# A warm-up of zeros, an attention's parts in another order, softmax steps in pairs and unpadded diagonal blocks

## The chip, the cores and the metric

The kernel runs on one core of a Trainium2 chip. The metric is the device time of one execution in microseconds (us); smaller is better. The engines are TensorE (PE, its weight loads PEld), VectorE (DVE), ScalarE (ACT), GpSimd (POOL) and SyncE (SP, which only starts DMAs). They run side by side and wait for each other through semaphores.

## The reference

512 tokens of width 1024 go through three stages in float32. A first block with attention and a wide FFN, a gated linear attention (GLA) and a sparse attention with selected keys (DSA). What the change touches:

```
# first block
u = rmsnorm(h, g_mix_pre); z = u @ w_in        # w_in also holds the latents q_lat, kv_lat and k_rope
q = rmsnorm(q_lat) @ w_q_up; kv = rmsnorm(kv_lat) @ w_kv_up      # 8 heads of 64 + 32 (rope), v of 64
q_pe, k_pe = rope(q_pe), rope(k_rope)
ob = softmax(mask(q_full k_full^T * scale)) v                    # mask by chunks of 64
ya = (a_b * conv3(a_c * a_x)) @ w_a_out                          # the branch called conv_a
...
# second block, layer 0: GLA, 4 heads, q, k of 256, v of 512
S = S * decay + k^T v; o = q S + (lower triangle of q k^T) v
# second block, layer 1: DSA, 16 heads of 128, one key and one value for all
logits = (q k^T) * ATTN_SCALE on the 128 selected keys of each query
o = softmax(logits) v
# behind each layer
x = layer_norm(ALPHA * x + y); x = x + (p @ ple_w) * sigmoid(x @ ple_gate_w)
```

## The kernel before

All activations lie transposed, features on partitions and 512 tokens in the free dimension, in eight tiles X[:, c, :]. A product in float32 is made of three matmuls in fp32r: each operand is split into a high part (a rounded copy, made by ACT) and a low part (the rest, made by DVE), and PE adds hi x hi, hi x lo and lo x hi (`part`, `mm3`, the L245 and L264 to L266 rows). Weights come as slabs of 128 x 1024 floats through four buffers called raw, and are split into whi and wlo in the same way. PSUM has banks for four uses: mm (3), s (2), t (2) and o (1).

PE's instructions stand in the order in which the code writes them. The other engines' instructions are put in order by a scheduler, so an edit of PE's order moves rows on DVE, ACT and POOL too. SP, ACT and POOL each issue DMAs in their own order.

**The start.** Five loads of X and of w_lat alternate on SP's queue; vec (all small vectors, 128 x 281) goes through ACT's. ACT makes XH as X times the gain column of vec, DVE makes XL. The latents need 72 matmuls, nine for each of the eight chunks.

**The first attention.** `Stream` holds the 24 half-steps of conv_a, 12 matmuls of 512 columns each, and `fill.run(n)` puts n of them between the attention's parts. kr is the key's rope part, r_u, rq and rk are reciprocal roots for 512 tokens, computed in [128, 4] tiles by chains of small DVE steps, and spread() brings such a tile into rows with transposes on PE. `mla_k` and `mla_q` make keys and queries of two heads, `mla_r` the rotated part of four heads' queries, which goes through DRAM (qrh, qrl) back into the tiles Qh and Ql by POOL's DMAs. `mla_s(h, t)` makes the scores of a query block t of 128, its maximum mx, the bias nb, the exponential p with its sum sm (ACT), the reciprocal and, on POOL, p times it. `soft_t` transposes p into bank t and splits it into pthi and ptlo, `mla_av` multiplies with V. The loop over eight heads does the transposes of head h, the scores of head h+1 and fill in turn.

**The padded blocks.** The last query block needs 128 columns. `weighted()` gives it 256 (three matmuls), with zeros ahead of it, and so do the scores of the first block in DSA:

```
c0 = min(j, 2) * 128
n = max(256, (t + 1) * 128)
```

**The tail.** The last tile of the last gate is computed at full width and then treated in two halves.

Of the kernel before, what the change touches and what calls it, by code (L numbers as in the profile page):

```python
# [96 lines left out]
def program(tc, a, out, upto=99):  # L97
# [72 lines left out]
    class Slab:  # L170


        def __init__(self, ap, cols):
            self.cols, self.parts = cols, []
            self.step = 512 if cols % 384 else 384
            self.raw = wp.tile([128, 1024], F32, name="raw", tag="raw", bufs=4)
            with tc.high_priority(offset=AHEAD):
                nc.sync.dma_start(self.raw[:, :cols], ap)

        def split(self, n=2):  # L180

# [100 lines left out]
    drp = top.enter_context(tc.tile_pool(name="drp", bufs=1, space=bass.MemoryType.DRAM))  # L282
    vec = cp.tile([128, NVEC], F32, name="vec")
# [8 lines left out]

    copy(cp.tile([128, 1], F32, name="warm"), ones)
# [8 lines left out]
    X = cp.tile([128, DC, S], F32, name="X")  # L302
# [159 lines left out]
    def weighted(ps, m, vs, pt):  # L462
# [6 lines left out]
    def soft_exp(p_, src, scale, nb, sm, eng=dve):  # L469

        act.activation(p_, src, AF.Exp, bias=nb, scale=scale, accum_out=sm)
        dve.reciprocal(sm, sm)
        eng.tensor_scalar(p_, p_, sm, None, op0=OP.mult)

    def soft_t(p_, t, pt):

        n = (t + 1) * 128
        ps = bank("t")
        for j in range(t + 1):
            pe.transpose(ps[:, j * 128:(j + 1) * 128], p_[:, j * 128:(j + 1) * 128], ident)  # L480
        pv = ps[:, :n].rearrange("p (j c) -> p j c", c=128)
        hi, lo = pt_view(pt[0], t), pt_view(pt[1], t)
# [75 lines left out]
    xin, w_in = a["xT"], a["w_in"]  # L558

    w_first = []  # L560
    for c0, c1 in ((0, 1), (1, 2), (2, 4), (4, 6), (6, 8)):
        with tc.high_priority(offset=AHEAD):
            nc.sync.dma_start(X[:, c0:c1, :], xin[:, c0 * S:c1 * S].rearrange("p (a b) -> p a b", b=S))
        w = slab(a["w_lat"][:, c0 * 384:c1 * 384], (c1 - c0) * 384)
        for i in range(c0, c1):
            split(XH[:, i, :], XL[:, i, :], X[:, i, :], vcol("g_mix_pre", i))
# [138 lines left out]
    fill.run(4)  # L705


# [3 lines left out]

    V = ap_.tile([128, NB, 8, 128], F32R, name="V")
    wv = slab(a["w_kv_v"], 1024)
    for b in range(NB):
        ps = bank("s" if b % 2 else "mm")
        bl = slice(b * 128, (b + 1) * 128)
        mm3(ps, [((kvn[k][0][:, bl], kvn[k][1][:, bl]),
                  wv(k * 512, 512)) for k in range(2)])
        split(V[:, b, :, 0:64], V[:, b, :, 64:128], ps[:, :].rearrange("p (h c) -> p h c", c=64), rk[:, b:b + 1])

# [32 lines left out]
    def mla_s(h, t):  # L753
        (qh, ql), (kh, kl) = QT[h % 2], KT[h % 2]
        if t == 0:
            MX[h] = [small(n_ + str(h % 2)) for n_ in ("mx", "nb", "sm")]
        mx, nb, sm = (x[:, t:t + 1] for x in MX[h])
        bl = slice(t * 128, (t + 1) * 128)
        n = max(256, (t + 1) * 128)
        ps_ = bank("s")  # L760
        pe.matmul(ps_[:, :n], qh[:, bl], kh[:, :n], start=True, stop=False)
        pe.matmul(ps_[:, :n], qh[:, bl], kl[:, :n], start=False, stop=False)
        pe.matmul(ps_[:, :n], ql[:, bl], kh[:, :n], start=False, stop=True)
        n = (t + 1) * 128
        dve.tensor_reduce(mx, ps_[:, :n], AX.X, OP.max)
        mul(nb, mx, nsrq[:, t:t + 1])
        p_ = PR[h, t] = ap_.tile([128, n], F32, name=f"p{t}", tag=f"p{t}")
        soft_exp(p_, ps_[:, :n], srq[:, t:t + 1], nb, sm, gps)
# [16 lines left out]
    mla_k(0)  # L785
    mla_q(0)
    fill.run(1)
    for t in range(NB):
        mla_s(0, t)
        if t == 1:  # L790
            mla_r(1)
# [911 lines left out]
```

## Time and profile before

| what | value |
|---|---|
| median of the runs | 1760.61 us (1759.82 to 1761.05, 3 runs) |
| the profiled execution | 1759.98 us |
| its span | 1758.2 us |
| PE busy | 1738.3 us, 8845 matmuls |
| DVE, ACT, POOL busy | 1207.0, 900.9, 86.6 us |
| first matmul | 5.96 us |
| PE's waits from 37 to 175 us | 7.6 us |

The span is what the profiler saw from the first to the last instruction; the time of the execution is 1.8 us longer. Ends of matmuls are modelled, since they are pipelined: how fast PE goes is read from the distance of the starts.

### The profile page before, as it was taken

The page shows a single profiled execution, that of the slowest core. Times are in us where ns is not written, and L with a number is a line of the kernel's source. Part 1 is how long each engine was busy: PE and PEld are TensorE (multiplying, and loading weights), DVE is VectorE, ACT ScalarE, POOL GpSimd, SP SyncE. Part 2 cuts the span into 40 slices and gives each one's busy share as a digit, 9 for nine tenths or more (in the row PEclk, how much of TensorE's full clock was granted, in tenths as well). Part 3 has the DMA queues.
Part 4 walks back from the last instruction along what each step waited for, and adds up shares of the span by engine and source line. Part 5 has one row for each costly group of instructions (what it writes and reads, how often), then busy time and mean ns, then how long its engine had stood idle before and what let it go on. Part 6 is the DMA issues. An engine that isn't in the chain of part 4 may idle for free.

```text
span 1758.2 us, 24149 instructions
## 1 busy us (share of the span) xinstructions
PE 1738.3 (99%) x8845; PEld 1464.7 (83%) x8845; DVE 1207.0 (69%) x2710; ACT 900.9 (51%) x1708; POOL 86.6 (5%) x147
## 2 busy tenths in 40 slices
PE   8899999999999999999999999999999999999998
PEld 6688888898888888899888888888988888888897
DVE  6987545488727657688554464556979988888885
ACT  6466433356434434455773744733765356444454
POOL 0455000000000000000000000000000000000000
PEclk9999999999999999999999999999999999999999
DMA  5322322213323232333312322232232321221231
GB/s 200 95 85 73 120 96 96 96 61 120 96 96 93 75 108 87 99 118 123 103 59 67 96 84 84 73 126 91 80 126 72 97 84 61 61 73 61 66 103 60
DMA packets 50758, 160.99 MB, mean 92 GB/s; under 512 B 5888, under 2 KB 7168, under 8 KB 50640
## 3 DMA queue, kind: packets, MB, share of 16 engines
q1 hardware_dynamic: 49328, 157.41, 27.5%
q0 software_dynamic: 1024, 1.64, 0.4%
q8 instruction: 69, 1.13, 0.3%
q14 instruction: 49, 0.40, 0.1%
q10 hardware_dynamic: 288, 0.41, 0.1%
HBM read 153.14 MB, written 4.72 MB: 90 GB/s over the span
## 4 chain that ended last, share of the span: by engine, by line
PE 96%; DVE 2%; ACT 1%; DMA 1%; issue 0%; SPq 0%; DVEq 0%; ACTq 0%
PE ps_mm L245 72%; PE ps_s L245 7%; PE ps_o L467 2%; PE ps_mm L264 2%; PE ps_mm L266 2%; PE ps_mm L265 2%; PE ps_t L480 1%; PE ps_s L467 1%; PE ps_t L1215 1%; PE ps_t L378 1%; PE ps_s L1161 1%; PE ps_o L777 1%; PE ps_s L264 1%; PE ps_s L265 1%; PE ps_s L266 1%; PE ps_t L340 0%
## 5 line engine op out<-in xcount | busy, mean ns | idle before, releaser
L116 ACT ACTIVATE whi<-raw 128x512 fp32r<-128x512 f32 (+1 forms) x551 | 337.4, 621 | 444.9 <-PE ps_mm L245 371.0
L245 PE MATMUL ps_mm<-XH,whi 128*128 128x512 f32 (+1 forms) x1376 | 522.9, 380 | 6.7 <-ACT whi L116 6.0
L245 PE MATMUL ps_mm<-XH,wlo 128*128 128x512 f32 (+1 forms) x1376 | 523.4, 380 | 0.2 <-DVE up L116 0.2
L245 PE MATMUL ps_mm<-XL,whi 128*128 128x512 f32 (+1 forms) x1376 | 522.0, 379 | 0.0
L116 DVE TENSOR_TENSOR wlo<-raw,whi 128x512 fp32r<-128x512 f32 (+2 forms) x549 | 368.7, 680 | 169.9 <-ACT whi L116 165.9
L245 PEld LDWEIGHTS ps_mm<-XH,whi 128*128 128x128 f32 x1376 | 259.9, 189 | 57.3 <-ACT whi L116 6.0
L245 PEld LDWEIGHTS ps_mm<-XL,whi 128*128 128x128 f32 x1376 | 260.0, 189 | 52.6
L245 PEld LDWEIGHTS ps_mm<-XH,wlo 128*128 128x128 f32 x1376 | 260.0, 189 | 51.7 <-PE ps_o L245 0.6
L116 ACT ACT_TABLE_LOAD x62 | 79.5, 1283 | 10.5 <-DVE nb L116 3.7
L116 DVE SCALAR_TENSOR_TENSOR upt<-up,vec,upt 128x511 f32<-128x511 f32 (+1 forms) x88 | 65.4, 749 | 10.9 <-ACT upt L116 9.7
L245 PE MATMUL ps_mm<-fh,wlo 128*128 128x512 f32 (+1 forms) x153 | 55.9, 365 | 0.0
L245 PE MATMUL ps_mm<-fh,whi 128*128 128x512 f32 (+1 forms) x153 | 55.8, 365 | 0.0
L245 PE MATMUL ps_mm<-fl,whi 128*128 128x512 f32 (+1 forms) x153 | 55.8, 365 | 0.0
L245 PE MATMUL ps_s<-XL,whi 128*128 128x256 f32 (+2 forms) x176 | 51.9, 295 | 0.7 <-DVE XL L116 0.7
L245 PE MATMUL ps_s<-XH,wlo 128*128 128x256 f32 (+2 forms) x176 | 51.8, 294 | 0.0
L245 PE MATMUL ps_s<-XH,whi 128*128 128x256 f32 (+2 forms) x176 | 51.4, 292 | 0.0
L116 DVE TENSOR_TENSOR up<-ps_mm,RU 128x512 f32<-128x512 f32 x41 | 28.2, 690 | 33.4 <-PE ps_mm L245 33.4
L266 PE MATMUL ps_mm<-whi,XL 128*128 128x512 f32 x128 | 50.6, 395 | 0.0
L264 PE MATMUL ps_mm<-whi,XH 128*128 128x512 f32 x128 | 50.6, 395 | 0.0
L265 PE MATMUL ps_mm<-wlo,XH 128*128 128x512 f32 x128 | 50.6, 395 | 0.0
L245 PE MATMUL ps_mm<-dth,wlo 128*128 128x512 f32 (+1 forms) x128 | 48.4, 378 | 0.0
L245 PE MATMUL ps_mm<-pthi,wlo 128*128 128x512 f32 (+1 forms) x128 | 48.2, 377 | 0.0
(506 smaller groups left out, 3217.2 us busy)
## 6 DMA issues: line engine op xcount, KB each, us to landing
raw<-in_w_ffn_up SPq DMA_DIRECT2D x44, 512.0 KB, 3.4
raw<-in_dsa_w SPq DMA_DIRECT2D x38, 512.0 KB, 3.5
raw<-in_w_in SPq DMA_DIRECT2D x31, 512.0 KB, 3.3
raw<-in_gla_qk SPq DMA_DIRECT2D x16, 512.0 KB, 4.3
raw<-in_gla_z SPq DMA_DIRECT2D x16, 512.0 KB, 3.5
raw<-in_gla_v SPq DMA_DIRECT2D x16, 512.0 KB, 3.5
raw<-in_gla_w_out SPq DMA_DIRECT2D x16, 512.0 KB, 3.4
raw<-in_ple_gate_w SPq DMA_DIRECT2D x16, 512.0 KB, 3.6
```

What stands on the lines that cost most here:

```text
L116: r = f(*args, **kw).ins
L245: pe.matmul(ps[:m, cs], l_, r_, start=(k == 0 and i == 0), stop=(k == n - 1 and i == 2))
L264: pe.matmul(ps, lh, rh, start=(i == 0), stop=False)
L265: pe.matmul(ps, lh, rl, start=False, stop=False)
L266: pe.matmul(ps, ll, rh, start=False, stop=(i == n - 1))
L378: pe.matmul(ps[:, b * 128:(b + 1) * 128], r.to_broadcast([128, 128]), ident, start=True, stop=True)
L467: pe.matmul(ps[:m, c0:], vs[j][a_], r[b_], start=(j == 0 and i == 0), stop=(j == NB - 1 and i == 2))
L480: pe.transpose(ps[:, j * 128:(j + 1) * 128], p_[:, j * 128:(j + 1) * 128], ident)
L777: pe.matmul(ps_[:m, c0:], V[:, j, h, 0:m], r_[i], start=(n == 0), stop=(n == len(steps) - 1))
L1161: pe.matmul(ps_[:, :384], g_[:, b, c * 128:(c + 1) * 128], dech, start=(i == 0), stop=(i == 1))
L1215: pe.matmul(ps_[:, bi], l_, r_, start=(c == 0), stop=(c == 1))
```

## The change

It has five parts.

1. Start: a tile of zeros, `idle`, and eight matmuls of 512 columns with it into bank o. The gain of the first norm comes as g_first, 128 x 8, by itself; it and the first weights w0 are loaded by ACT's queue, X's first tile by SP's. w0 is rounded by DVE instead of ACT.
2. Order of the first attention: see the diff; conv_a's half-steps are dealt out in another way, and V stands behind the first keys, mla_r(1) in the loop at head 1.
3. Softmax in MLA and DSA: nb and the reciprocal are computed for two query blocks in one instruction; the exponentials stay apart.
4. The last 128-block in GLA and DSA (not in the first attention) is multiplied by one matmul of 128 x 128 in float32 instead of three of 256 columns in fp32r. It takes raw copies of the operands (gvr, dvr, dkr, dqr, ptr, a third diag tile) instead of split ones. The same holds for DSA's scores of the first block.
5. Tail: the last gate tile's projection is computed in two halves of 256 columns, and each half is treated behind its own matmuls.

```diff
     def split(self, n=2, copy=copy):
...
+    X = cp.tile([128, DC, S], F32, name="X")
+    g_first = cp.tile([128, DC], F32, name="g_first")
+    with tc.high_priority(offset=AHEAD):
+        nc.sync.dma_start(X[:, 0, :], xin[:, 0:S])
+        nc.scalar.dma_start(g_first, a["vec"][:, :DC])
+    w0 = Slab(a["w_lat"][:, 0:384], 384, nc.scalar)
...
+    idle = cp.tile([128, S], F32R, name="idle")
+    dve.memset(f32v(idle), 0.0)
+    ps = bank("o")
+    for _ in range(8):
+        pe.matmul(ps, idle[:, 0:128], idle, start=True, stop=True)
...
-            for j in range(NB):
+            for j in range(n):
                 c0, r = pt_terms(pt, j)
                 pe.matmul(ps[:m, c0:], vs[j][a_], r[b_], start=(j == 0 and i == 0), stop=(j == NB - 1 and i == 2))
+        if last is not None:
+            pe.matmul(ps[:m, S - 128:], *last, start=False, stop=True)
...
+        for i, (p_, src, scale) in enumerate(zip(ps, srcs, scales)):
+            act.activation(p_, src, AF.Exp, bias=nb[:, i:i + 1], scale=scale, accum_out=sm[:, i:i + 1])
         dve.reciprocal(sm, sm)
-        eng.tensor_scalar(p_, p_, sm, None, op0=OP.mult)
+        for i, p_ in enumerate(ps):
+            eng.tensor_scalar(p_, p_, sm[:, i:i + 1], None, op0=OP.mult)
...
-    fill.run(4)
+    kr = Folded(w_in[2]).proj(xs)
+    fill.run(1)
+    copy(rub, spread(r_u))
...
+    fill.run(2)
 
     copy(rkb, spread(rk))
...
     mla_r(0)
     mla_k(0)
+    V = ap_.tile([128, NB, 8, 128], F32R, name="V")
...
+    fill.run(1)
     mla_q(0)
+    fill.run(2)
+    mla_s(0, (0, 1))
     fill.run(1)
-    for t in range(NB):
-        mla_s(0, t)
-        if t == 1:
-            mla_r(1)
+    mla_s(0, (2, 3))
     fill.run(1)
     for h in range(8):
...
         if h < 7:
-            mla_s(h + 1, 2)
-            mla_s(h + 1, 3)
+            mla_s(h + 1, (2, 3))
+        if h == 1:
+            mla_r(1)
         if h < 6 and h % 2 == 0:
             mla_k(h // 2 + 1)
             mla_q(h // 2 + 1)
-        fill.run(1 if h < 7 else 99)
+        fill.run((2, 0, 2, 0, 2, 1, 1, 99)[h])
         mla_av(h, pt)
...
+            if t == 0:
+                pe.matmul(ps_[:, :n], qr, KR, start=True, stop=True)
+            else:
+                mm3(ps_[:, :n], [((qh[:, bl], ql[:, bl]), (KH[:, :n], KL[:, :n]))])
...
+        for i, ps_ in rows(w_ap, 0, DC - last, xs, pss):
+            gated(i, ps_, FULL)
+        if last:
+            w = slab(w_ap[DC - 1], 1024)
+            for cs in HALVES:
+                gated(DC - 1, proj(w, 0, xs, cs=cs), cs)
```

Three places show what the change moves. The first is ACT's queue at the start, its loads (L178, L284, L289, L292) and its first copies. Before:

```order
L284 DMA vec<-in_vec 128x281
L116 ACT_TABLE_LOAD
L116 ACTIVATE warm<-ones 128x1
L116 ACTIVATE XH<-X,vec 128x512
L116 ACTIVATE whi<-raw 128x384
```

And of the change:

```order
L178 DMA raw<-in_w_lat 128x384
L289 DMA g_first<-in_vec 128x8
L292 DMA vec<-in_vec 128x281
L116 ACT_TABLE_LOAD
L116 ACTIVATE warm<-ones 128x1
L116 ACTIVATE XH<-X,g_first 128x512 x2
```

The first copy of weights leaves ACT for DVE, and vec stands behind two other loads.

The second place is PE behind the latents, where ru and the sums acc_q and acc_kv of the norms are brought over by transposes (ps_t). Before, they follow kr's products at once, and 48 L245 rows of fill stand between them and the transposes of rk_r:

```order
L229 MATMUL ps_mm<-XH,whi 128x512
L378 MATMUL ps_t<-con,ru 128x128 x4
L340 MATMUL ps_t<-ones,acc_q 128x1 x4
L340 MATMUL ps_t<-ones,acc_kv 128x1 x4
L245 MATMUL ps_mm<-XH,whi 128x512
```

In the change, where L378 and L340 have become L391 and L353:

```order
L245 MATMUL ps_mm<-XH,wlo 128x512
L391 MATMUL ps_t<-con,ru 128x128 x4
L353 MATMUL ps_t<-ones,acc_q 128x1 x4
L353 MATMUL ps_t<-ones,acc_kv 128x1 x4
L245 MATMUL ps_mm<-XH,whi 128x512
```

Twelve L245 rows of fill now stand ahead of the ru transposes and 24 between the acc_kv row and those of rk_r.

The third place is the loop at head 3, on PE, in the change: transposes of p (head 3, blocks 2 and 3), scores of head 4 (blocks 2 and 3), and the first products with V.

```order
L499 MATMUL ps_t<-con,p_1221 128x128 x4
L264 MATMUL ps_s<-Kh_405,Qh_409 128x384
L265 MATMUL ps_s<-Kl_406,Qh_409 128x384
L266 MATMUL ps_s<-Kh_405,Ql_410 128x384
L264 MATMUL ps_s<-Kh_405,Qh_409 128x512
L265 MATMUL ps_s<-Kl_406,Qh_409 128x512
L266 MATMUL ps_s<-Kh_405,Ql_410 128x512
L793 MATMUL ps_o<-pthi,V 128x512
```

Before, 12 matmuls of fill stand between such scores and the products with V; at this head they are gone. On DVE the same place reads, in the change:

```order
L116 RECIPROCAL sm_1342<-sm_1342 128x2
L116 TENSOR_TENSOR ptlo<-ps_t,pthi 128x3x128
L116 TENSOR_TENSOR ptlo<-ps_t,pthi 128x4x128
L116 TENSOR_REDUCE mx_1340<-ps_s 128x1 x2
L116 SCALAR_TENSOR_TENSOR X<-ac,vec,X 128x511
L116 TENSOR_TENSOR nb_1341<-mx_1340,nsrq 128x2
L116 TENSOR_TENSOR ot<-ps_o,ou 64x512
```

And before, at the same head:

```order
L116 TENSOR_REDUCE mx_1283<-ps_s 128x1
L116 TENSOR_TENSOR ptlo<-ps_t,pthi 128x3x128
L116 TENSOR_TENSOR ptlo<-ps_t,pthi 128x4x128
L116 TENSOR_TENSOR nb_1284<-mx_1283,nsrq 128x1
L116 TENSOR_REDUCE mx_1283<-ps_s 128x1
L116 TENSOR_TENSOR nb_1284<-mx_1283,nsrq 128x1
L116 RECIPROCAL sm_1285<-sm_1285 128x1 x2
```

One nb for two blocks follows both maxima and a step of the convolution; before, each block's nb stands behind its own maximum.

## Rows read from the trace of the kernel before

**Rows 1.** The page's first part: busy us of each engine, share, instructions.

```profile
PE 1738.3 (99%) x8845; PEld 1464.7 (83%) x8845; DVE 1207.0 (69%) x2710; ACT 900.9 (51%) x1708; POOL 86.6 (5%) x147
```

**Rows 2.** Windows: stretch, length, busy PE, PEld, DVE, ACT, POOL; clock, DMA, GB/s.

```profile
100.00:175.00 75.00, 73.34 (x388) 61.08 (x387) 60.89 (x149) 52.39 (x122) 40.02 (x50) 1.00 0.26 80
175.00:1750.00 1575.00, 1573.86 (x8070) 1331.53 (x8069) 1066.51 (x2379) 790.53 (x1477) 15.67 (x53) 1.00 0.28 89
```

**Rows 3.** PE's waits, 37 to 175 us: us in total, times, longest.

```profile
PE ps_s L761 <- ACT p L116: 3.7, 7, 1.2
PE ps_s L761 <- DMA Qh<-qrh: 1.9, 1, 1.9
...
PE ps_t L340 <- DVE rq_v L116: 0.3, 1, 0.3
```

**Rows 4.** Windows again, around two waits.

```profile
46.00:49.40 3.40, 3.40 (x9) 2.65 (x9) 3.40 (x19) 0.00 (x0) 0.00 (x0) 0.50 0.00 0
76.60:80.10 3.50, 3.18 (x11) 2.58 (x11) 3.40 (x8) 0.41 (x1) 1.14 (x1) 0.52 0.51 133
```

**Rows 5.** Timeline of the start: start us, us, engine, line, operation, idle before.

```profile
4.77 0.72 ACT L116 ACTIVATE XH<-X,vec 128x512 fp32r<-128x512 f32 x1 [2.03 <-DMA vec<-in_vec]
5.96 0.79 PE L245 MATMUL ps_mm<-XH,whi 128*128 128x512 f32 x1 [5.96 <-ACT whi L116]
9.96 0.92 ACT L116 ACTIVATE whi<-raw 128x384 fp32r<-128x384 f32 x2
11.24 0.63 PE L245 MATMUL ps_mm<-XH,whi 128*128 128x512 f32 x1
12.23 0.39 PE L245 MATMUL ps_mm<-XH,whi 128*128 128x512 f32 x1
25.52 0.40 PE L245 MATMUL ps_s<-XH,whi 128*128 128x512 f32 x1
```

**Rows 6.** A DMA issue: count, KB, us from issue to landing.

```profile
con<-in_con POOLq DMA_DIRECT2D x1, 3.5 KB, 4.6
```

**Rows 7.** Timeline of DVE: first and last step of rk's chain.

```profile
45.45 0.16 DVE L116 SCALAR_TENSOR_TENSOR rk_v<-ps_t,ru 128x4 f32<-128x4 f32 x1 [0.73 <-PE ps_t L340]
...
52.80 0.16 DVE L116 TENSOR_TENSOR rk_r<-rk,ru 128x4 f32<-128x4 f32 x1
```

**Rows 8.** The loop: timeline rows, then POOL's groups from 100 to 175 us.

```profile
141.91 1.14 DVE L116 TENSOR_TENSOR ptlo<-ps_t,pthi 128x384 fp32r<-128x384 f32 x2
142.97 1.14 DVE L116 TENSOR_REDUCE mx<-ps_s 128x1 f32<-128x384 f32 x2
144.27 0.67 ACT L116 ACTIVATE p<-ps_s,nb,srq 128x384 f32<-128x384 f32 x1 [0.42 <-DVE nb L116]
154.74 0.74 DVE L116 SCALAR_TENSOR_TENSOR X<-ac,vec,X 128x510 f32<-128x510 f32 x1
L473 POOL TENSOR_SCALAR p<-p,sm 128x512 f32<-128x512 f32 x6 | 9.8, 1637 | 0.8 <-PE ps_o L777 0.7
L473 POOL TENSOR_SCALAR p<-p,sm 128x384 f32<-128x384 f32 x6 | 8.0, 1330 | 8.9 <-DVE sm L116 8.3 <-DVE nb L116 0.6
L699 POOL TENSOR_TENSOR X<-X 128x512 f32<-128x512 f32 x2 | 2.6, 1288 | 0.0
```

**Rows 9.** L1215 alone: its window, its loads (min/median/max ns); then two rows of DSA's scores.

```profile
873.57:877.95 4.38, 4.38 (x40) 4.38 (x39) 1.00 0.79 251
L1215 PEld LDWEIGHTS ps_t<-ex x64: 187/192/193, 873.3 to 1174.2; 128*128 128x128 f32 x64
1510.33 0.28 PE L264 MATMUL ps_s<-dkh,dqh 128*128 128x256 f32 x1
1510.45 0.28 PE L265 MATMUL ps_s<-dkl,dqh 128*128 128x256 f32 x1
```

**Rows 10.** Timeline of the tail, behind the last matmul.

```profile
1753.15 0.66 ACT L116 ACTIVATE pg<-ps_mm 128x256 f32<-128x256 f32 x2 [5.01 <-PE ps_mm L245]
1754.24 0.75 DVE L116 TENSOR_TENSOR X<-X,pg 128x256 f32<-128x256 f32 x2
```

More of the change, by code (lines that the diff above doesn't have):

```diff
@@ L480, in soft_t @@
             pe.transpose(ps[:, j * 128:(j + 1) * 128], p_[:, j * 128:(j + 1) * 128], ident)
+        if t == NB - 1 and last is not None:
+            copy(last, ps[:, n - 128:n])
+            t, n = t - 1, n - 128
         pv = ps[:, :n].rearrange("p (j c) -> p j c", c=128)
-        hi, lo = pt_view(pt[0], t), pt_view(pt[1], t)
+        hi, lo = pt_view(pt[0], t0, t + 1), pt_view(pt[1], t0, t + 1)
         copy(hi, pv)
@@ L704, in program @@
     fill = Stream(sum((conv_a(c) for c in range(4)), []))
-    fill.run(4)
+    kr = Folded(w_in[2]).proj(xs)
+    fill.run(1)
+    copy(rub, spread(r_u))
+    mul(rub2, rub, rub)
+    srq = small("srq")
+    nsrq = small("nsrq")
+    rq = latent(accq, 384, "rq")
+    dve.tensor_scalar(srq, rq, QK_SCALE, None, op0=OP.mult)
+    dve.tensor_scalar(nsrq, rq, -QK_SCALE, None, op0=OP.mult)
+    rk = latent(acck, 256, "rk")
+    krl, krs = tmp("krl"), tmp("krs")
+    r = slice(0, 64)
+    copy(krl[r, :], kr[64:128, :])
+    add(krs[r, :], kr[r, :], krl[r, :])
+    kpe = rope(krs, r)
+    r = ROPE[1]
+    mul(kpe[r, :], kpe[r, :], rub[r, :])
+    copy(KT[1][0][r, :], kpe[r, :])
+    copy(KT[0][0][ROPE[0], :], kpe[r, :])
+    for par in (1, 0):
+        sub(KT[par][1][ROPE[par], :], kpe[r, :], f32v(KT[1][0][r, :]))
+    fill.run(2)
     copy(rkb, spread(rk))
@@ L710, in program @@
     kvn = [(KVH[:, i, :], KVL[:, i, :]) for i in range(2)]
[L712 to L719, printed above, removed]
     OBH = m1.tile([128, 4, S], F32R, name="OBH")
@@ L751, in mla_q, with mla_s @@
             split(QT[par][0][NOPE[par], :], QT[par][1][NOPE[par], :], ps_[NOPE[par], :])
-    def mla_s(h, t):
+    def mla_s(h, ts):
         (qh, ql), (kh, kl) = QT[h % 2], KT[h % 2]
-        if t == 0:
+        if ts[0] == 0:
             MX[h] = [small(n_ + str(h % 2)) for n_ in ("mx", "nb", "sm")]
[L757 to L768, printed above, removed]
+        two = slice(ts[0], ts[-1] + 1)
+        mx, nb, sm = MX[h]
+        srcs = []
+        for t in ts:
+            bl = slice(t * 128, (t + 1) * 128)
+            n = max(256, (t + 1) * 128)
+            ps_ = bank("s")
+            mm3(ps_[:, :n], [((qh[:, bl], ql[:, bl]), (kh[:, :n], kl[:, :n]))])
+            n = (t + 1) * 128
+            srcs.append(ps_[:, :n])
+            dve.tensor_reduce(mx[:, t:t + 1], ps_[:, :n], AX.X, OP.max)
+            PR[h, t] = ap_.tile([128, n], F32, name=f"p{t}", tag=f"p{t}")
+        mul(nb[:, two], mx[:, two], nsrq[:, two])
+        soft_exp([PR[h, t] for t in ts], srcs, [srq[:, t:t + 1] for t in ts], nb[:, two], sm[:, two], gps)
     def mla_av(h, pt):
@@ L1120, in program @@
     dg = []
-    for i in range(2):
+    for i in range(3):
         t_ = gq.tile([128, 128], F32, name=f"diag{i}")
@@ L1191, in gla_v @@
         mm3(ps_, terms, DC // 2, DC)
-        split(vh[:, b, :], vl[:, b, :], ps_)
+        if b == NB - 1:
+            copy(vr, ps_)
+        else:
+            split(vh[:, b, :], vl[:, b, :], ps_)
     def gla_z(h, i):
@@ L1532, in program @@
     PR, MX = {}, {}
-    for t in range(NB):
-        dsa_s(0, t)
-        if t == 1:
-            dsa_z(12)
+    dsa_s(0, (0, 1))
+    dsa_z(12)
+    dsa_s(0, (2, 3))
     ts = None
@@ L1540, in program @@
     for h in range(16):
-        pt = pt_tiles(tp, 1)
+        pt = pt_tiles(tp, 1, 1280, False)
+        last = tp.tile([128, 128], F32, name="ptr", tag="ptr")
         for t in (0, 1):
@@ L1563, in program @@
             steps[0]()
-        dsa_av(h, pt)
+        dsa_av(h, pt, last)
         if h == 15:
```

170 lines of the change are left out of this document (83 added, 87 removed).

## The prediction

> **What bounds the kernel now.** I read the page's busy times first: PE works 1738.3 of a span of 1758.2 us [rows 1]. Then I cut the span into stretches. From 175 us to 1750 us PE is busy for 1573.86 of 1575 us at the full clock; in the first attention's loop, 100 to 175, for 73.34 of 75, and there DVE is busy for 60.89 and ACT for 52.39 [rows 2]. So behind 175 us only less TensorE work saves time, and a vector operation added or removed there is worth nothing while PE doesn't wait. Ahead of 175 us waits count too. PE's waits from 37 to 175 us sum to 7.6 us in six rows (3.7, 1.9, 0.7, 0.7, 0.3, 0.3), and half of it is scores that wait for an exponential to free their bank [rows 3]. They cost a second time: behind two of these waits the granted clock is at half (0.50 for 3.40 us, 0.52 for 3.50 us, so 1.2 GHz of 2.4) [rows 4]. Half of that time is lost, 1.7 + 1.6 = 3.3 us. At the start, the first matmul runs at 5.96; twelve start by 11.24, 0.44 us apart, three more by 12.23, and from there 57 by 25.52, 0.233 apart. A matmul's own time goes from 0.63 to 0.39 with it [rows 5], as when half a clock becomes a whole one. The change comes near 11.9, when PE has worked since 5.96.
>
> **A, the start.** The zeros need only a memset, and DVE has nothing else to do, so PE can begin near 1.5 (an estimate). If zeros do for the clock what data did, the pitch changes as much later, at 7.4. Real work needs g_first, X's first tile and the first weights. g_first is 128 rows of 32 B, issued on ACT's queue behind w0, some 0.4 later than vec was. vec was there at 4.77 [rows 5], so g_first lands at 5.1 or later; the nearest small transfer, con of 3.5 KB, takes 4.6 us [rows 6], which from 1.2 on (an estimate of its issue) is 5.8. With 0.72 for XH behind it [rows 5] the first product runs between 5.8 and 6.5, where it was 5.96; I take 6.1. So the shorter vector brings nothing. The Trainium skill speaks against it too ("DMA: Bandwidth & Descriptors", Specifications): transfers under 512 B do a read-modify-write; the row of con agrees in that 3.5 KB took 4.6 us, and the sum by the page would be that of the late end, 0.4 us less.
> From 6.1 on: three products at 0.44 to 7.4, the other 15 of the first two chunks at 0.233 to 10.9; the third chunk's weights are copied from 9.96 to 10.9 [rows 5] and their low parts follow on DVE, so that it starts near 11.2; 54 more at 0.233 end at 23.8. Before they ended at 25.5: **+1.7**. Bounds: -0.5 if the zeros do nothing for the clock and g_first is late, +2.3 if no weight holds PE up.
>
> **B, keys, values and the first head.** mla_r(0), its rotations and its DMAs through POOL now stand ahead of V (24 matmuls), 12 of fill, mla_q and 24 more, so the waits for Qh, Ql and rot go, and with longer fills between the score pairs the waits for p in the first heads too: all 7.6, and with them the 3.3 of clock. That is 10.9 to be had. What comes in: spread(rk) waits for the chain of small DVE operations from rk_v to rk_r, 45.45 to 52.96, 7.5 us long [rows 7]. PE had 48 matmuls of fill there and now has 24, 5.6 us at 0.233: a wait of 1.8 (0 if the chain is shorter with r_u's squares out of its way, 3 if DVE has the rope steps first). 0.4 for small seams, as two of the 0.3 kind remain [rows 3].
>
> **C, the loop.** Fills of (2,0,2,0,2,1,1) take cover from h=1, 3 and 7. I go through the heads where that, or a moved step, shows.
> At h=3 scores (2,3) stand straight ahead of av. From the transposes on DVE and ACT do the first pthi 0.5 (an estimate: a little under ptlo's half), ptlo 1.14, two maxima 1.14, a step of the conv that stands between, 0.74, nb as a small step [rows 7] 0.15 and the first exponential 0.67 [rows 8], 4.3 in all; the second's 0.77 (its columns are more) less PE's 0.35 between the banks adds 0.4, hand-overs 0.3: 5.0. PE has scores 1.2, av 1.3 and transposes 0.4 (columns at 0.233 for 512): 2.9. The wait is 2.1.
> At h=4 POOL scales the second pair: 0.77 + 0.15 until the sums are there, then X 1.29 of the conv, 1.33 and 1.64 [rows 8], 5.2, with hand-overs 5.8. PE has two short scores, 12 of fill and transposes, 4.1. The wait is 1.7.
> At h=2 the steps of mla_r(1), now in the loop, stand in DVE's queue ahead of the maxima, 128x512 sums of some 0.7 each as the conv's 0.74 [rows 8]; two aren't covered: 1.4. Behind them stand head 3's exponentials and POOL's copies.
> At h=7 the fills are used up and av follows its own transposes: both pthi, about 1.0 (ptlo is 1.14 [rows 8]), and hand-overs: 1.2.
> Together 6.4, with one in four that a wait halves the clock once more (3.3): 0.8. New waits 1.8 + 0.4 + 6.4 + 0.8 = 9.4 for the 10.9 removed: **+1.5** for B and C. Bounds: +8 if slack in the queues swallows the loop's waits, -4 if they are twice as long (12.8 + 3.0). The pairs' joint nb and reciprocal take 32 operations of 0.15 from DVE here, 4.9 us in all, but hold the first exponential back by one maximum; I leave it at nothing, since both lie in DVE's slack of 14 of 75 us [rows 2].
>
> **D, unpadded blocks.** 16 blocks in GLA's av, 16 in DSA's av, 16 in DSA's first scores: 48 places where three matmuls of 256 columns, 0.117 each (1510.33, 1510.45), become one fp32 matmul of 128 columns. The nearest rows for that are GLA's scores: 20 such matmuls (40 records) in 4.38 us, 0.219 each [rows 9]. 48 x (0.351 - 0.219) = **+6.3**, all of it on PE in the stretch where PE is the bound. Lower bound: two weight loads of 0.192 one behind the other [rows 9], 0.384, a loss of 1.6. The Trainium skill ("FP8 and Floating Point Precision", TensorE Precision Notes) gives true FP32 four passes through the array; four times 128 columns are the 0.233 of a 512-column product, and the sum by that is 5.7, an estimate from that page. The row, 0.219, is close under it and stands. The extra copies (KR, VR, dqr, ptr) and the memsets that go are ACT's, DVE's and POOL's in a stretch where these work 790.53, 1066.51 and 15.67 of 1575 us [rows 2]: nothing; if PE waited there they would cost some 0.3 each.
>
> **E, the tail.** Before, sigmoid, product and sum of both halves followed the last matmul, the sigmoids 0.66 and the sums 0.75 for two [rows 10], the products about as long. Now the first half's chain runs while PE computes the second, and one half's 0.33 + 0.38 + 0.37 stays: the last sum ends at 1754.23 and not at 1754.99. +0.76, less 0.1 for the smaller matmuls: **+0.6** (0 to 0.8).
>
> **The sum.** 1.7 + 1.5 + 6.3 + 0.6 = 10.1 from the profiled execution's 1759.98 (span 1758.2 and 1.8 around it) is 1749.9. That execution lies 0.6 under the median of the runs, 1760.61, so I forecast **1750.5**. No change can be told from noise within 0.2%, 3.5 us.
>
> **The rivals.** First: the waits are really emptied: the loop's queues run early enough that only 3 us of the 9.4 come. For it: DVE and ACT are idle for 14 and 23 of 75 us. Against: at h=3 and 7 nothing lies between. 6.4 less: 1744.1.
> Second: the zeros don't bring the clock forward, or data limits the start anyway: A is 0. For it: no row shows what zeros do for the clock. 1752.2.
> Third: the fp32 matmul between fp32r ones costs its two loads. For it: PEld is busy for all of the 4.38 us [rows 9]. Against: these two loads overlapped in it. D is -1.6: 1758.4, no measurable change.
> Fourth, slower: the pair's scores need both s banks, and both stay taken until a joint nb behind two maxima; that happens at seven heads. Its price per head is the maxima 1.14, the late first exponential 0.67 and a stalled fill, about 3.0 [rows 8], 21 where I have 6.4, and the clock falls at one (3.3 where I have 0.8): 17 more, 1767.6. It decides from 2.9 us a head on with the clock still up: 20 for 6.4 eats 10.1 and the 3.5 besides. For it: DVE at 81% in the loop [rows 2]. Against: bank waits there were 3.7 in seven so far [rows 3], at most 1.2.
>
> **How the numbers follow.** My forecast 0.45, the first rival 0.30, the second 0.13, the third 0.05, the fourth 0.07. The range takes the forecast's bounds for A (half of it), B and C up to the first rival, and the second: 1743.5 to 1756.5. Outside lie rivals 3 and 4 and a strip of 0.06 below. Faster by over 0.2%: the first three, 0.88; within: the third and the near part of the fourth, 0.07; slower 0.05.
>
> **What would show it.** PE's rows at the start: eight with idle, then pitch 0.233 from near 7.4, first product near 6.1. PE's waits from 37 to 175: none for Qh or p in the first head, one of some 2 us ahead of the L391 transposes for spread(rk), one each near heads 3, 4 and 7. GLA's and DSA's stretches shorter by 6 us with PE as busy as before. Wrong would be: a new clock of 0.5 in the loop, PE waits behind 175 us, the fp32 matmul's pitch above 0.3, or the pitch of the start unchanged.

## The result and the profile after

The changed kernel takes 1741.38 us (median of 4 runs, 1739.97 to 1742.81) against 1760.24 for the kernel before: a ratio of 0.9892, 95% interval 0.9879 to 0.9905, 18.9 us faster where 10.1 were forecast and 17.1 was the most that the range allowed (1743.5 against the 1760.61 that it set out from). The profiled execution took 1742.37, its span is 1740.3.

The page's first part, as [rows 1]: PE is busy for 23 us less, with nearly as many matmuls.

```profile
PE 1715.0 (99%) x8829; PEld 1461.0 (84%) x8829; DVE 1192.8 (69%) x2607; ACT 899.7 (52%) x1736; POOL 78.4 (5%) x108
```

Where the time went is read from the starts of three matmuls, us from the span's start, in the profiled executions of all kernels told of below:

```
kernel                          first kr   first CH   last matmul
before                             25.52     189.73       1752.71
after                              25.05     198.22       1735.70
e1  before, moved 32 bytes         24.63     187.80       1730.31
e2  after, moved back              23.72     197.98       1756.69
e3  after, old order               24.89     188.71       1726.22
e4  after, no zeros                25.59     198.30       1735.80
e5  after, old loop                23.41     191.12       1728.64
e6  before, moved 96 bytes         24.72     188.32       1733.08
e7  before, moved 160 bytes        24.82     190.49       1746.70
e8  e3, all operands alike         25.14     190.29       1719.42
e9  e8, all moved 128 bytes        24.43     189.27       1718.33
e10 e8, 14 zeros                   23.34     188.25       1717.85
e11 new start, more fill           24.98     189.21       1718.25
e12 e8, single steps               25.19     188.35       1717.45
f1  f2, padded                     23.49     188.29       1723.57
f2  e8, 14 zeros, single steps     23.40     188.22       1717.36
f3  before, all operands alike     24.55     187.69       1722.30
```

kr follows the 72 latent matmuls, CH is the first operand behind the first attention. In the profiled executions, after against before: 0.5 us gained to kr, 9.0 *lost* from kr to CH, 25.5 gained from CH to the last matmul, 0.9 behind it; 17.9 of the span in all. The 9.0 are mostly parts B and C (e3 below). The 25.5 are far more than the 6.3 forecast for part D, and most of them have a cause that the forecast did not contain. The groups by line and form (count, busy us, mean ns of one) show it, first three of the kernel before:

```profile
L245 PE MATMUL ps_mm<-XH,whi 128*128 128x512 f32 x1168 | 464.4, 398 | 6.7 <-ACT whi L116 6.0 <-DVE rot L116 0.7
L264 PE MATMUL ps_mm<-whi,XH 128*128 128x512 f32 x128 | 50.6, 395 | 0.0
L245 PE MATMUL ps_mm<-fh,whi 128*128 128x512 f32 x111 | 44.0, 397 | 0.0
```

and of the changed kernel:

```profile
L245 PE MATMUL ps_mm<-XH,whi 128*128 128x512 f32 x1160 | 453.4, 391 | 1.3 <-ACT XH L116 1.3
L264 PE MATMUL ps_mm<-whi,XH 128*128 128x512 f32 x128 | 49.9, 390 | 0.0
L245 PE MATMUL ps_mm<-fh,whi 128*128 128x512 f32 x111 | 43.7, 394 | 0.0
```

The same matmuls, whose code nobody touched, are some 6 ns shorter, those with XH and XL and those that stream weights past XH. The chain of waits gives it as distances: in the GLA stage (start, length), 24 products with XH take 5.60 before and 5.44 after, 0.233 and 0.227 each. Of the kernel before:

```profile
883.91 1.94 PE ps_s L467 x12
885.97 5.60 PE ps_mm L245 x24
```

Of the changed kernel, where the first row is a product of part D, 9 fp32r matmuls and, in the gap behind them, one in fp32:

```profile
882.83 1.58 PE ps_s L482 x9
884.75 5.44 PE ps_mm L245 x24
```

From the start of one row to that of the next the product takes 1.92 and not 2.06: part D shortens it by 0.14, about the 0.132 that the forecast gives to one place.

PE's waits from 37 to 200 us, in answer to [rows 3]. Those for Qh, Ql, ru and rq_v are gone, that for rot is down from 0.7 to 0.2, and with the new ones they sum to 15.6 where 7.6 stood:

```profile
PE ps_t L391 <- DVE rk_r L116: 7.3, 1, 7.3
PE ps_s L264 <- ACT p L116: 5.2, 4, 2.4
PE ps_t L499 <- POOL p L492: 1.6, 3, 0.8
PE ps_o L793 <- ACT pthi L116: 0.7, 1, 0.7
PE ps_t L499 <- DVE ptlo L116: 0.6, 1, 0.6
PE ps_mm L264 <- DVE rot L116: 0.2, 1, 0.2
```

Windows around the low clock, in answer to [rows 4] (PE busy, PEld, DVE, ACT, POOL; clock, DMA share, GB/s). It is at half, 1.2 of 2.4 GHz, for 17.1 us in all. 6.8 of them begin during the wait for rk, when PE had stood still since 51.6, and the two in the loop begin at 124.1 and 148.0, behind waits that end at 124.1 and 146.4. Two signs that the prediction named for being wrong are there: a new half clock in the loop, and waits of PE behind 175 us, since the loop ends later:

```profile
8.00:11.40 3.40, 3.40 (x10) 2.63 (x9) 2.85 (x5) 3.40 (x8) 0.00 (x0) 0.50 1.02 400
55.80:62.60 6.80, 3.72 (x13) 3.36 (x14) 6.51 (x16) 1.20 (x2) 6.55 (x9) 0.50 0.37 99
124.00:127.50 3.50, 3.43 (x9) 2.96 (x10) 2.28 (x6) 0.56 (x3) 0.92 (x2) 0.51 0.42 131
148.00:151.40 3.40, 3.40 (x10) 2.63 (x9) 2.51 (x6) 0.68 (x3) 3.21 (x2) 0.50 0.00 0
```

The start and the tail, in answer to [rows 5, 6, 10]: g_first's transfer (KB, us to landing), then rows of the timeline.

```profile
g_first<-in_vec ACTq DMA_DIRECT2D x1, 4.0 KB, 4.3
1.55 3.51 PE L305 MATMUL ps_o<-idle 128*128 128x512 f32 x8 [1.55 <-DVE idle L116]
6.40 0.50 PE L245 MATMUL ps_mm<-XH,whi 128*128 128x512 f32 x1 [1.33 <-ACT XH L116]
1736.01 0.38 ACT L116 ACTIVATE pg<-ps_mm 128x256 f32<-128x256 f32 x1 [2.49 <-PE ps_mm L245]
1736.89 0.42 DVE L116 TENSOR_TENSOR X<-X,pg 128x256 f32<-128x256 f32 x1
```

### The profile page after: what moved, and what is told of

It reads as the page before. It is cut to its first block, busy times and chain, and to the rows that moved or that the text cites. A ratio compares the mean times of both kernels' runs of the same rounds, so it can differ in the third digit from the quotient of the medians.

```text
span 1740.3 us, 23988 instructions
## 1 busy us (share of the span) xinstructions
PE 1715.0 (99%) x8829; PEld 1461.0 (84%) x8829; DVE 1192.8 (69%) x2607; ACT 899.7 (52%) x1736; POOL 78.4 (5%) x108
## 4 chain that ended last, share of the span: by engine, by line
PE 94%; DVE 3%; ACT 1%; issue 1%; DMA 1%; POOL 1%; ACTq 0%; DVEq 0%
PE ps_mm L245 70%; PE ps_s L245 7%; PE ps_o L482 2%; PE ps_mm L264 2%; PE ps_mm L265 2%; PE ps_mm L266 2%; PE ps_t L499 1%; PE ps_s L264 1%; PE ps_s L266 1%; PE ps_s L265 1%; PE ps_t L1251 1%; PE ps_t L391 1%; PE ps_s L1193 1%; PE ps_s L482 1%; PE ps_o L793 0%
## 5 line engine op out<-in xcount | busy, mean ns | idle before, releaser
L245 PE MATMUL ps_mm<-XH,wlo 128*128 128x512 f32 (+1 forms) x1384 | 519.2, 375 | 0.3 <-DVE up L116 0.3
L245 PE MATMUL ps_mm<-XH,whi 128*128 128x512 f32 (+1 forms) x1384 | 516.7, 373 | 1.3 <-ACT XH L116 1.3
L245 PE MATMUL ps_mm<-XL,whi 128*128 128x512 f32 (+1 forms) x1384 | 516.7, 373 | 0.3 <-DVE XL L116 0.3
L245 PEld LDWEIGHTS ps_mm<-XL,whi 128*128 128x128 f32 x1384 | 261.4, 189 | 47.0 <-DVE XL L116 0.6
L245 PEld LDWEIGHTS ps_mm<-XH,whi 128*128 128x128 f32 x1384 | 261.7, 189 | 46.0 <-ACT XH L116 1.8
L245 PEld LDWEIGHTS ps_mm<-XH,wlo 128*128 128x128 f32 x1384 | 261.5, 189 | 45.3 <-PE ps_o L245 0.7
L116 DVE SCALAR_TENSOR_TENSOR upt<-up,vec,upt 128x511 f32<-128x511 f32 (+1 forms) x88 | 65.5, 750 | 10.7 <-ACT upt L116 9.5
L245 PE MATMUL ps_mm<-fh,wlo 128*128 128x512 f32 (+1 forms) x153 | 55.5, 363 | 0.0
L245 PE MATMUL ps_mm<-fh,whi 128*128 128x512 f32 (+1 forms) x153 | 55.4, 362 | 0.0
L245 PE MATMUL ps_mm<-fl,whi 128*128 128x512 f32 (+1 forms) x153 | 55.4, 362 | 0.0
L245 PE MATMUL ps_s<-XL,whi 128*128 128x256 f32 (+2 forms) x176 | 52.0, 295 | 0.6 <-DVE XL L116 0.6
L245 PE MATMUL ps_s<-XH,wlo 128*128 128x256 f32 (+2 forms) x176 | 51.9, 295 | 0.0
L245 PE MATMUL ps_s<-XH,whi 128*128 128x256 f32 (+2 forms) x176 | 51.4, 292 | 0.0
L116 ACT ACTIVATE pthi<-ps_t 128x384 fp32r<-128x384 f32 (+1 forms) x104 | 40.3, 416 | 16.0 <-PE ps_t L499 15.8
L245 PE MATMUL ps_mm<-ptlo,whi 128*128 128x512 f32 (+1 forms) x128 | 48.1, 376 | 0.3 <-DVE ptlo L116 0.2
L245 PE MATMUL ps_mm<-dth,wlo 128*128 128x512 f32 (+1 forms) x128 | 48.4, 378 | 0.0
```

The costliest lines, as they stand in the source:

```text
L116: r = f(*args, **kw).ins
L245: pe.matmul(ps[:m, cs], l_, r_, start=(k == 0 and i == 0), stop=(k == n - 1 and i == 2))
```

## Experiments

**The place in memory.** A tile's place is its byte address within a partition, as the built program lists it. Before, XH stood at 75616, 96 bytes past a multiple of 256; the weights' halves stand 128 past one in all kernels but e9. The change puts X ahead of vec, and behind it g_first with 32 bytes and idle with 2048. XH then stands at 77696, 128 past a multiple: g_first's 32 bytes are the difference. The first two runs move nothing but this. e1 adds a line to the kernel before (e2 the same with 24 floats, to the changed kernel):

```diff
+    cp.tile([128, 8], F32, name="pad")
     XH = cp.tile([128, DC, S], F32R, name="XH")
```

In brackets behind a time stand its ratio to the kernel before, which ran beside it, and the 95% interval.

> The kernel before with nothing but an unused tile of 32 bytes a partition allocated ahead of XH, so that XH, XL and all that is allocated behind them move by 32 bytes; XH then starts at a multiple of 128 bytes, as in the changed kernel, where it started 96 bytes past one. Theory (the place of the operands in memory sets the pitch of the matmuls): the 512-column matmuls with XH, XL or a weight slab as the moving operand go from 0.233 to 0.227 apart, 3900 of them by 0.0058 are 22 us, the 256-column ones with XH lose 0.003 each, 3 us; 1760 becomes 1741 to 1743. Rival (the pitch follows from the changed instructions): pitch 0.233 and 1760 as before.

> The changed kernel with an unused tile of 96 bytes ahead of XH, so that XH starts 96 bytes past a multiple of 128 again. Theory of the place in memory: pitch back to 0.233, 1741 becomes 1759 to 1762, so the change without it is worth nothing within 0.2%. Rival: 1741, pitch 0.227.

e1 took 1737.87 (0.9873, 0.9858 to 0.9888): 22.5 us from an unused tile, more than the whole change brings. In e1 and in the changed kernel the tiles that the matmuls of the table below read start at the same places in 256 bytes; at equal places the change is 3.5 us slower (1741.38 against 1737.87, and the slowest run of e1, 1737.92, is under the fastest of the other, 1739.97). e2 took 1763.56 (1.0021, 1.0011 to 1.0030): without its place in memory the change makes the kernel 0.2% slower, though e2's places, 224 and 160 in the table, are not those of the kernel before. The groups of e1, then of e2:

```profile
L245 PE MATMUL ps_mm<-XH,whi 128*128 128x512 f32 x1168 | 457.2, 391 | 6.8 <-ACT whi L116 6.1 <-DVE rot L116 0.7
L264 PE MATMUL ps_mm<-whi,XH 128*128 128x512 f32 x128 | 49.9, 390 | 0.0
```

```profile
L245 PE MATMUL ps_mm<-XH,whi 128*128 128x512 f32 x1160 | 458.9, 396 | 0.9 <-ACT XH L116 0.9
L264 PE MATMUL ps_mm<-whi,XH 128*128 128x512 f32 x128 | 50.7, 396 | 0.0
```

The mean goes with the place, both ways. Which place it has to be, the next runs ask: e6 and e7 with 96 and 160 bytes in e1's line, e8 with the old order of e3 (below) and the pools behind XL and at the other end of memory moved too, e9 with everything of e8, the weights too, 128 bytes further on.

```diff
     XL = cp.tile([128, DC, S], F32R, name="XL")
+    cp.tile([128, 16], F32, name="pad")
...
+    top.enter_context(tc.tile_pool(name="padr", bufs=1, side="right")).tile([128, 24], F32, name="padr")
```

and for e9, beside a padr of 56 floats,

```diff
+    top.enter_context(tc.tile_pool(name="pad0", bufs=1)).tile([128, 32], F32, name="pad0")
     wp = top.enter_context(tc.tile_pool(name="wp", bufs=4, reuse_waits="tile"))
```

In these texts and in f3's the third run is e3, and the run before e9 is e8.

> The kernel before with 96 bytes ahead of XH: now XH and XL start 64 bytes past a multiple of 128, and fh, fl, CH, MH, QNH and most of pthi, which lie in the pools behind, start at one. Theory (both operands at multiples of 128 give the shorter pitch): XH stays at 0.233, fh, pthi and the others, some 1100 matmuls of 512 columns, go to 0.227, 6 to 7 us: 1753 to 1755. Rival (something about XH's own place, or a shift by any amount): no gain, 1760, or 1738 as with 32 bytes.

> The kernel before with 160 bytes ahead of XH, so that XH starts at a multiple of 2048, where with 32 bytes it started 128 short of one. If multiples of 128 are what counts: 1738, pitch 0.227, as with 32 bytes. If it is the distance to the weights' tiles (which start 128 past a multiple of 256) or a larger multiple: another time, 1760 at the far end.

> The changed kernel with the old order, as in the third run, and two unused tiles more, of 64 bytes behind XL and of 96 at the other end of memory, so that nearly every operand of the matmuls starts at a multiple of 128. Theory of the place in memory: 1750 more matmuls of 512 columns get the shorter pitch, 10 us, less 1 to 2 for 256-column ones, which were closer together at 64 past: 1724 to 1726. Rival: 1733, as in the third run.

> The kernel of the run before this (old order, all operands at the same place in 256 bytes as the weights, 128) with everything, the weights too, 128 bytes further on. Over the runs so far the short pitch, 0.227, came wherever the moving and the stationary operand both start 128 bytes past a multiple of 256, and 0.229 to 0.234 came at all other pairs. If the two need only the same place in 256 bytes: 1724 as before this shift. If the place itself counts: pitch 0.230 to 0.234 for 5700 matmuls, 20 to 35 us more, 1744 to 1759.

e6 took 1740.44 (0.9883, 0.9867 to 0.9900), e7 1753.29 (0.9955, 0.9941 to 0.9970). e6 is outside every range given, and multiples of 128 are not the rule; of e7's two cases the second holds, the distance to the weights' tiles. e8 took 1724.02 (0.9791, 0.9777 to 0.9806), as expected, and e9 1724.19 (0.9795, 0.9780 to 0.9810): the place itself doesn't count, the two operands' distance does. The distance of successive starts of 512-column matmuls against the weights, about 3500 with XH or XL and 465 with fh or fl (the hidden activations of the FFN) as the moving operand, the one whose columns stream past the stationary one, medians worked out from each trace, beside each tile's start in 256 bytes:

```
        weights   XH, XL: start, ns    fh, fl: start, ns    median us
before    128          96  233              32  234          1760.2
e2        128         224  232             160  234          1763.6
e7        128           0  232             192  229          1753.3
e6        128         192  229             128  227          1740.4
after     128         128  227              64  233          1741.4
e1        128         128  227              64  233          1737.9
e8        128         128  227             128  227          1724.0
e9          0           0  227               0  227          1724.2
```

Equal starts in 256 bytes give 227; a moving operand 64 bytes past the stationary one gives 229; all others 232 to 234. A multiple of 512 is not needed: in e8 the weights start 128 past one, fh too, XH 384 past one, and both give 227. In e6, where fh has the good place and XH the second best, the groups say the same; where the roles change (second row) the moving weights lie 64 short of XH, and the mean is that of the kernel before:

```profile
L245 PE MATMUL ps_mm<-XH,whi 128*128 128x512 f32 x1168 | 459.2, 393 | 6.5 <-ACT whi L116 5.8 <-DVE rot L116 0.7
L264 PE MATMUL ps_mm<-whi,XH 128*128 128x512 f32 x128 | 50.6, 395 | 0.0
L245 PE MATMUL ps_mm<-fh,wlo 128*128 128x512 f32 x111 | 43.2, 390 | 0.0
```

By means, e1's gain is about 3500 x (0.2332 - 0.2275) = 20.0 for XH and XL, 384 x 0.006 = 2.3 for weights that stream past XH, and the 1091 products of 256 columns with XH lose 0.0015 each, 1.6: 20.7 of the 22.5 measured.

f3 asks what the kernel before gets from three unused tiles alone (e1's line and the two of e8).

> The kernel before with three unused tiles alone, of 32 bytes ahead of XH, 64 behind XL and 96 at the other end of memory, so that nearly all operands of the matmuls start at the same place in 256 bytes as the weights. By the pitch of the runs so far: the 22.5 that 32 bytes brought and 9 more as in the aligned kernel with the old order: 1728 to 1730.

It took 1729.19 (0.9824, 0.9809 to 0.9838), 31.3 us less than before without a changed instruction, and 12 less than the changed kernel.

**Parts B and C.** e3 undoes the order and the fills, XH staying where the change put it; e5 the loop alone.

```diff
-    fill.run(2)
+    fill.run(4)
     copy(rkb, spread(rk))
...
+    mla_r(1)
...
-        fill.run((2, 0, 2, 0, 2, 1, 1, 99)[h])
+        fill.run(1 if h < 7 else 99)
```

> The changed kernel with the first attention's order and fills of before (parts B and C undone; softmax in pairs, unpadded blocks, start and tail kept, XH at its multiple of 128). By the forecast B and C gained 1.5: slower, 1743. By the trace of the changed kernel, where the end of the attention's loop comes 8.5 us later than before in spite of the shorter pitch, B and C lose about 11: faster, 1730 to 1732, and the first product of the next stage starts near 187.

> The changed kernel with part C alone undone: one half-step of fill at each place of the loop again, and the second rotation between the score pairs of the first head; the start of the attention (part B) stays as changed. If the loop without cover is what costs, as the forecast has it (6.4 of new waits there), most of the 9.5 between the changed kernel and the one with the old order comes back: 1733 to 1736. If the waits for rk (7.3 us and a halved clock of 6.8 us behind them) are the larger part, less than half comes back: 1737 to 1740.

e3 took 1733.16 (0.9846, 0.9832 to 0.9861), 8.2 less than the changed kernel; e5 1736.32 (0.9861, 0.9847 to 0.9876), 5.1 less. So the loop costs 5.1 and the start of the attention 3.2; from kr to CH the traces say 5.5 and 3.9. e5 lies between the two ranges of its expectation: the loop is the larger part, 5.1 of 8.2, but not nearly all. Its waits (0 to 200 us, those above 2) show what the old loop leaves, the wait for rk and one for POOL at the end, each with a stretch of half clock that begins in it (52.9 to 59.8 and 179.2 to 182.6); why POOL is late there no run asks:

```profile
PE ps_t L391 <- DVE rk_r L116: 6.2, 1, 6.2
PE ps_s L264 <- ACT p L116: 3.2, 5, 0.9
PE ps_t L499 <- POOL p L492: 3.0, 1, 3.0
```

Why rk is late, the changed kernel's timeline shows, DVE and ACT from 44 to 59 us:

```profile
44.77 0.43 DVE L116 CAST pos<-posi 128x512 f32<-128x512 int32 x1 [2.66 <-DMA posi<-in_pos]
47.89 0.15 DVE L116 SCALAR_TENSOR_TENSOR rq_v<-ps_t,ru 128x4 f32<-128x4 f32 x1
49.89 0.15 DVE L116 SCALAR_TENSOR_TENSOR rk_v<-ps_t,ru 128x4 f32<-128x4 f32 x1
55.06 0.68 DVE L116 TENSOR_TENSOR krs<-ps_mm,krl 64x512 f32<-64x512 f32 x1 [1.30 <-ACT krl L116]
58.16 0.57 DVE L116 TENSOR_TENSOR rk_r<-rk,ru 128x4 f32<-128x4 f32 x1
52.49 1.28 ACT L116 ACT_TABLE_LOAD   x1 [3.20 <-DVE rq L116]
54.44 0.59 ACT L116 ACTIVATE krl<-ps_mm 64x512 f32<-64x512 f32 x1
```

rk's chain takes 8.8 us from rk_v to rk_r, against 7.5 before [rows 7], and it starts 4.4 later, 3.9 behind the end of the transposes that feed it (46.0): the angles for the rotation, which wait for posi until 44.77, stand ahead of rk_v on DVE, and krs, a step of the key's rope that the change moved beside the chain, holds DVE while ACT loads a table and copies krl. e11 gives that place four half-steps of fill, all operands alike, the loop old.

```diff
-    fill.run(2)
+    fill.run(4)
     copy(rkb, spread(rk))
...
+    mla_q(0)
     fill.run(1)
-    mla_q(0)
-    fill.run(2)
     mla_s(0, (0, 1))
+    mla_r(1)
```

> The aligned kernel with the changed start of the attention (rope, keys, values ahead of the queries), four half-steps of fill ahead of the transposes of rk instead of two (fewer behind V and mla_q), and the old loop. Theory: the wait of 7.3 us for rk and the halved clock behind it came from too little fill, so that 5.4 of fill more leave 1 to 2 of the wait and no low clock; the waits for Qh that the old order has (2.1) don't come back: 1719 to 1722, against 1724 for the old order. Rival: the waits move on (to p of the first heads, or V), 1723 to 1726.

It took 1723.21 (0.9791, 0.9776 to 0.9805), no other than e8's 1724.02. The wait for rk falls to 0.5, further than expected, but not the sum; its waits of over 1 us behind the start:

```profile
PE ps_s L265 <- ACT p L117: 3.6, 5, 0.9
PE ps_t L501 <- POOL p L494: 3.0, 1, 3.0
PE ps_mm L265 <- DVE rot L117: 2.8, 1, 2.8
```

The next consumer of the same late DVE work, V's products, which wait until DVE's rot steps are through, takes the wait over (2.8, from 62.06), as the rival had it, and the half clock that the theory had ruled out comes behind it (66.0 to 69.4). That DVE's order is the cause is read from these traces; no run moves the angles behind rk's chain.

**Parts A and D, and the pairs.** e4 drops the zeros (range 0 in their loop), e10 takes 14, e12 calls the softmax for one block at a time, f2 joins e10 and e12, f1 is f2 with the padded blocks of before.

```diff
-    for _ in range(8):
+    for _ in range(14):
         pe.matmul(ps, idle[:, 0:128], idle, start=True, stop=True)
...
-            mla_s(h + 1, (0, 1))
+            mla_s(h + 1, (0,))
+            mla_s(h + 1, (1,))
...
-        weighted(ps_, 128, [(VH[:, j, :], VL[:, j, :]) for j in range(NB - 1)], pt, (VR, last))
+        weighted(ps_, 128, [(VH[:, j, :], VL[:, j, :]) for j in range(NB)], pt)
```

> The changed kernel without the eight matmuls of zeros (the tile and its memset stay). By the forecast the zeros gain 1.7: 1743. By the trace after, where the clock rises at 4.6 us and falls back to half from 8.0 to 11.4 us, they bring at most 0.5: 1741 to 1742, and the first 72 products end within 0.5 us of the 25.05 of the changed kernel.

> The aligned kernel with the old order, with 14 matmuls of zeros instead of 8, so that they reach the first data at 6.4 us. If the gap between the zeros and the data is why the clock was low from 8 to 11.4 us in some executions and high in others: the clock stays up from near 5, the products with kr start at 23.4 to 23.7 and not at 25.1, and the time is 1722.5. If the zeros don't hold the clock whatever their number: 1724 and 25.1.

> The aligned kernel with the old order and the small softmax steps for one block at a time, as before the change, in both attentions. The forecast put the pairs at nothing: 1724. If a joint nb holds the first exponential back (PE's waits for p are 4.6 there against 4.0 with single steps): 0.5 to 1 less in the first attention, 1723.

> The aligned kernel with the old order, single softmax steps and 14 zeros: what the runs so far leave of the change. If the gains add (1.2 of the zeros, 1.9 of single steps, by the stretches of their traces): 1721 to 1722, and the attention's loop ends near 186.5. If one eats the other: 1723 to 1724.

> The aligned kernel with the old order, single softmax steps and 14 zeros, with part D undone: the last blocks padded to 256 columns and in three matmuls again. Against the next run this is D alone. By the forecast's prices (0.351 against 0.219, 48 times) it is 6.3 slower than that; by the stretches of the runs so far, where the kernel with unpadded blocks was 4.9 shorter behind the first attention, tail included, 5 slower; if the fp32 matmuls bring nothing, equal. 1726.5 to 1728.

e4 took 1740.72 (0.9887, 0.9871 to 0.9904), no other than the changed kernel. Its kr starts at 25.59, 0.5 later, but that this is the zeros' doing is not shown: with the same eight, kr starts between 23.41 (e5) and 25.19 (e12). PE's rows take three courses there. In the changed kernel, e3 and e11 the matmuls double their pace at the last zeros, 4.6 to 4.7, PE has nothing from 5.1 to 6.3 or 6.4, and near 8.0 the granted clock falls to half for 3.4 us (kr at 24.89 to 25.05). In e2 and e5 all eight zeros are slow, the data run at the full pace from the first, and the clock stays up (23.72, 23.41). In e8, e9 and e12 the zeros and the data are slow until 9 to 10.7, with starts 0.43 apart, although the granted clock reads 1.00 there, as it does in the slow start of the kernel before (kr at 24.43 to 25.19). What decides between them no run shows. With 14 zeros and no gap the pace stayed up in all three traces (e10, f2, f1: kr at 23.34, 23.40, 23.49), 1.8 us ahead of e8 and 1.2 ahead of f3, which has the old start and equal places. By the time e10 (1723.21; 0.9788, 0.9772 to 0.9804) and e8 can't be told apart. e12 took 1723.80 (0.9792, 0.9778 to 0.9807), f2 1723.62 (0.9789, 0.9773 to 0.9805): single steps bring nothing that shows; the 2 us from kr to CH by which e12's profile is shorter than e8's are not there between f2's and e10's (164.8 and 164.9), and e8's has a third stretch of half clock (82.7 to 86.1) that e12's lacks.

f1 took 1728.25 (0.9820, 0.9805 to 0.9835): part D is worth 4.6 by the medians, 6.1 by the two traces from CH to the last matmul; f1's trace is of its slowest run, 1729.93.

## Why the prediction was wrong

**The step that failed** is in the first part: that behind 175 us only less TensorE work saves time. Every sum there takes 0.233 us for a 512-column matmul as fixed, so that all the matmuls that the diff leaves alone are put at nothing, without a reason. The price was a property of where two tiles lay. The change moved one by 32 bytes, and 3900 matmuls became 0.006 shorter: 22 us (e1, e2), which neither the forecast nor a rival had. That the time came out faster, as forecast, is luck: at equal places the change is 3.5 us slower (e1 against the changed kernel), and e2, 0.1 to 0.3% slower, lies on the side that was given 0.05. By parts, at equal places: A nothing that shows for +1.7, B and C -8.2 for +1.5, D 4.6 to 6.1 for +6.3, E +0.6 as forecast.

**B, keys, values and the first head: +10.9 to be had, 2.2 of new waits.** The 10.9 were right in kind: Qh, Ql, rot and ru are not waited for any more, but for rot's 0.2. The wait for rk was put at 1.8, at most 3, and is 7.3. The chain was priced where it stood before, with cover shortened; its start was taken as unmoved. It starts 4.4 later and runs 1.3 longer, in a trace where the angles and the moved rope steps stand among its steps on DVE, and half the clock follows for 6.8 us, 3.4 lost, where none was counted. The waits for p in the first heads were to go too; that for the first head's exponentials is 2.4 (85.02 to 87.45) where it was 1.2, in both behind a table load of ACT, 1.28, that the forecast did not look at.

**C, the loop: 6.4 of new waits and 0.8 for the clock.** The waits between 100 and 200 us sum to 5.8, by head 1.8 at h=2 (forecast 1.4), 1.5 at h=3 (2.1), 0.8 at h=4 (1.7), 0.5 at h=6, 1.3 at h=7 (1.2). In sum and in place that held, though h=4 has half of its wait. The clock fell twice, 3.4 lost. And these are not set off by the waits removed, which B's new ones ate. Together B and C were forecast as +1.5 and are -8.2 (e3). The fourth rival, 21 from a joint nb, is out: the loop's waits are 5.8, and e12 without joint steps is no faster.

**A: +1.7.** No gain shows in the changed kernel. Its kr is 0.5 earlier than before, but 72 matmuls at the shorter distance are 0.4 of that, and against e1, with the old start at equal places, it is 0.4 later; with one and the same start kr varies by more. The pace did rise with the zeros, at 4.6, where the forecast had 7.4. What the forecast left out is the gap between the zeros and the data: behind it the clock fell at 8.0. With 14 zeros and no gap the three traces keep the pace and are 1.1 to 1.2 ahead of f3. The first product came at 6.40, within the 5.8 to 6.5 given. g_first's 4.0 KB took 4.3 us, vec's 140.5 KB had taken 3.9 before: the shorter vector brings nothing, as the prediction said. The Trainium skill ("DMA: Bandwidth & Descriptors", Specifications) puts the least transfer for the full rate at 512 B, with a read-modify-write below that; the trace agrees in that rows of 32 B gained nothing.

**D: +6.3.** The mechanism held, the size is a little under: 4.6 by the medians of f1 and f2, 6.1 between their traces. The four passes of the Trainium skill ("FP8 and Floating Point Precision", TensorE Precision Notes) would have given an estimate of 5.7, which lies between them; these runs can't decide. The first and third rivals, emptied waits and fp32 at two loads, are out; the second, A at nothing, is what the changed kernel shows.

**E: +0.6.** 0.9 behind the last matmul (5.5 from its start to the span's end before, 4.6 after), and the 48 halves at 0.120 take 0.3 more than 24 whole ones at 0.227: 0.6. The pairs of small steps: nothing, as forecast.

## What to carry to other kernels

When a change allocates, moves or drops a tile, list the start addresses of the matmuls' operands before and after, modulo 256, and compare the distance of successive starts of untouched matmuls; in this kernel, where TensorE is busy for 99% of the time, that was the largest term. Before crediting a new order, undo it with the tiles kept in place. And cover, the work that PE does while a chain runs on another engine, must be measured against when that chain starts in the new order, not only how long it is.

The best version (f2, e8, e10 and e12 are equal by the time, and so is e11 with the new start of the attention) is the old order with unpadded blocks and all operands at equal starts: 1723 to 1724, 36.9 us under the kernel before, 31.3 of which f3 has from unused tiles alone.

## What was not expected of the hardware

The distance of 512-column fp32r matmuls depends on the two operands' starts modulo 256 bytes: 227 ns at equal starts, 229 with the moving one 64 past, 232 to 234 otherwise. The 256-column ones run the other way: with XH 117 at the old place and 120 at equal starts (medians), with fh 114 with the moving start 64 short of the weights' and 120 at equal ones. In the short groups of the attentions (dkh with dqh, pthi with gvh; 12 to 16 of each form) equal starts show no such gain, 229 to 236. Why this is so no run here shows; starts at distances other than those in the table were not tried. And with the same code at the start, kr began up to 1.8 us apart (23.41 in e5, 25.19 in e12), by how long the zeros and the first data ran at half pace and whether the granted clock fell again behind PE's gap of 1.3 us. The granted clock doesn't show all of it: it reads 1.00 from the first matmul, also where successive starts are 0.43 apart.
